# Attention scores of a hybrid block: two heads side by side on 64 rows of the array each, the causal mask added to the key terms by GpSimd

## The chip, the cores and the metric

The program runs on one core of a Trainium2 chip (8 cores, on two dies of four). The metric is the device time of one execution in microseconds (us). Lines L1, L2, ... are lines of the kernel's file, before the change unless the text says otherwise.

## The reference

Two blocks over 1024 tokens of width 1024, batch 1. All arrays are float32. The first block puts 16 learned tokens ahead of the sequence (1040 keys) and runs a state space model (SSD) and 16 heads of 64 of "forgetting" attention; the second runs 4 heads of differential attention (each with two parts of 64) and 8 heads of dilated attention of 64. What the change touches are the scores:

```python
# forgetting attention, c = cumulative sum of log f
s = jnp.einsum("bthd,bshd->bhts", qi, k).astype(jnp.float32) * scale
s = s + (cqi[..., :, None] - c_k[..., None, :])
s = jnp.where(kpos[None, :] <= qpos[:, None], s, -jnp.inf)
p = jax.nn.softmax(s, axis=-1).astype(v.dtype)
# differential attention: two parts c of each head
s = jnp.einsum('bqhce,bkhce->bchqk', qblk, k).astype(jnp.float32) * scale
s = s - slopes[:, None, None] * dist
a = jax.nn.softmax(s, axis=-1)
w = a[:, 0] - lam * a[:, 1]
# dilated attention: s + bias, masked, softmax, for three patterns that are merged
```

## The kernel before

**Numbers.** A float32 operand is kept as two halves, hi and lo, of a reduced float32 type (fp32r), and a product is the sum of hi*hi, hi*lo and lo*hi (`mm3`, L112 to L114). Projections (`project`) hold channels on the 128 partitions, so one strip of 128 weight columns gives the q, k or v of two heads: head 0 on partitions 0 to 63, head 1 on 64 to 127.

**Scores.** A head has 64 channels, half of the array's 128 rows. `stack_q` (L443, L444) splits a head's q or k into hi (ScalarE) and lo (VectorE), each head by instructions of its own on 64 partitions; `move_q` and `move_k` (L451, L457, L458) then copy halves by DMA to the other 64 partitions, so that one operand of 128 rows holds (hi, lo) of q, and two hold (hi, hi) and (lo, lo) of k. Two products of 128 rows give a head's scores: kx then ky (L566, L567; L1167; L1262 and L1264). Two heads take four products for each stretch of keys.

**Order.** `pipeline` writes the steps of eight query tiles of 128 tokens: A(i) are the scores, their maximum and the exponential, B(i) transposes the result (L620, L1289), C(i) multiplies by v (L599, L604, L1206, L1313). A runs two tiles ahead: A(i+2), C(i-1), B(i). `merge` interleaves these with the projections of the gate and of the next pair of heads by nominal costs, so the order on each engine is fixed when the program is built. Every engine takes its instructions in that order, and one that waits holds all behind it.

**Forgetting attention (`fox_attend`, eight pairs of heads).** Tile i sees W = 16 + 128(i+1) keys, 144 to 1040, in chunks of at most 512 columns. VectorE (L570) reads a chunk from PSUM, adds the key terms `cb` (the cumulative log gates, loaded by L543 as 1040 columns on all partitions for each head) and takes the running minimum of the negated scores; ScalarE (L573) takes the exponential. The causal mask of the last 128 columns is a third product: identity times a matrix of large numbers in bf16 (L569), added in PSUM. At the start of a pair, SyncE issues the store of the pair before (L611, it waits for y of L606) and then the two loads of `cb`. GpSimd clears vz and puts the v of the first 16 keys there (`v_meta`, L477, L483); TensorE transposes it (L487), then v (L468), and then comes A(0).

**The second block.** The differential attention (`scores`, L1167) writes a tile's 1024 columns of one head to a pair of PSUM banks, of which the pool has two; VectorE (L1169) reads each whole pair of banks. The dilated attention (L1262, L1264) has 688 columns for each tile in two pieces, each in a bank of its own. q and k come there from `norms` in `pair_project`: normed, split, and moved by DMA. In the narrow products L599 and L1313 two heads already share the array: each uses 64 of its columns.

Of the kernel before, what the change touches and what calls it, by code (L numbers as in the profile page):

```python
# [17 lines left out]
T = 1024  # L18
# [48 lines left out]
class Kern:  # L67
# [16 lines left out]
    def half(self, name):  # L84
        """512 columns; in the tail from a pool of their own"""
        if self.halfs is None:
            return self.slot(name, w=512)
        return self.halfs.tile([128, 512], F32, tag="half", name=name, bufs=11)

    def psum(self, one, two):  # L90
        """the banks of PSUM from here on: single ones and pairs"""
        if self.psx:
            self.psx.close()
        self.psx = self.ctx.enter_context(ExitStack())
        self.ps = self.psx.enter_context(self.tc.tile_pool(name="ps", bufs=1, space=bass.MemoryType.PSUM))
        self.one, self.two = one, two
# [35 lines left out]
    # weight strips, in the order in which they are used  # L132
# [63 lines left out]
    def consts(self):  # L196
# [6 lines left out]
        self.identb = cst.tile([128, 128], BF16, name="identb")  # L203
        self.maskb = cst.tile([128, 128], BF16, name="maskb")
        V.tensor_copy(out=self.identb, in_=self.ident)
        V.tensor_copy(out=self.maskb, in_=self.cm[:, 3, :])
# [11 lines left out]
    def rstd(self, out, ss, n):  # L218
        """1 / sqrt(ss / n + eps)"""
# [9 lines left out]
    def rsqrt(self, v, pool):  # L229
        """v [128, n] > 0 in place to 1/sqrt(v): a first guess from the exponent, three Newton steps"""  # L230
# [29 lines left out]
    def token_sums_T(self, t, n):  # L260
        """the sums by tokens: [128 tokens, block of 128, part, 32]"""
# [5 lines left out]
    def rows_out(self, v, n, dst):  # L267
        """v [128 tokens, n = (row, block of 128)]: rows of 1024 tokens in DRAM"""
# [56 lines left out]
    def softplus(self, x):  # L325
        """x [128, 9, n] in place to max(x, 0) + log(1 + exp(-|x|)), the logarithm by the series of artanh"""
# [16 lines left out]
    def dt_f(self):  # L343
# [21 lines left out]
        # cumulative log forget gates (negated: csp), as rows  # L365
# [31 lines left out]
    def dt_ssd(self):  # L397
        """SSD: within-chunk cumulative a*dt, decays"""
# [34 lines left out]
    def stack_q(self, src, stacks, c0, c1, scale, perm=False):  # L433
        """src [128 = two heads x 64, n] fp32; head 0: rows (hi, lo), head 1: rows (lo, hi); with perm, the
        tokens in the order of classes modulo 4"""
        nc = self.nc
        dst = classes if perm else lambda x: x
        if perm:
            src = by_class(src)
# [7 lines left out]
    def move_q(self, stacks, n):  # L447
        for j, st in enumerate(stacks):
            a, b = ((0, 64), (64, 128))[j]
            o, p = ((64, 128), (0, 64))[j]  # L450
            self.nc.sync.dma_start(out=st[0][o:p, :n].bitcast(F32), in_=st[1][a:b, :n].bitcast(F32))  # L451

    def move_k(self, stacks, n):
        for j, st in enumerate(stacks):
            a, b = ((0, 64), (64, 128))[j]
            o, p = ((64, 128), (0, 64))[j]
            self.nc.sync.dma_start(out=st[0][o:p, :n].bitcast(F32), in_=st[1][a:b, :n].bitcast(F32))  # L457
            self.nc.sync.dma_start(out=st[1][o:p, :n].bitcast(F32), in_=st[0][a:b, :n].bitcast(F32))  # L458
# [33 lines left out]
    def fox_project(self, p, st):  # L492
        nc = self.nc
        k = [(self.slot("kx", F32R), self.slot("ky", F32R)) for _ in range(2)]
        yield from self.project(("k", p), self.u1, PIECES_L if p else PIECES_P,
                                lambda ps, c0, c1: self.stack_q(ps, k, c0, c1, 1.0))
        self.move_k(k, L)
        st["k"] = k
        q = [(self.slot("qs", F32R), self.slot("qt", F32R)) for _ in range(2)]
        yield from self.project(("q", p), self.u1, PIECES_T,  # L500
                                lambda ps, c0, c1: self.stack_q(ps, q, c0 - 16, c1 - 16, -0.125))
        self.move_q(q, T)
        st["q"] = [s[0] for s in q]
        del q
# [11 lines left out]
    def silu2(self, ps, out):  # L516
        """2 * silu"""
# [5 lines left out]
    def pipeline(n, A, B, C, pre=lambda i: None):  # L523
        """stages of each of n query tiles, the scores two tiles ahead"""
# [13 lines left out]
    def fox_attend(self, p, st):  # L538
        nc, te = self.nc, self.nc.tensor
        cb = []  # L540
# [10 lines left out]
        def A(i):  # L551
# [5 lines left out]
            Ns[i] = []  # L557
            for j in range(2):
                N = self.slot("N")
                mn = self.sm.tile([128, 3], F32, tag="mn", name="mn", bufs=4)  # L560
                qt = st["q"][j][:, i * 128:(i + 1) * 128]
                for c in range(n):
                    s0, s1 = c * w, min(W, c * w + w)
                    S = self.bank()[:, :s1 - s0]
                    last = c == n - 1
                    te.matmul(S, qt, st["k"][j][0][:, s0:s1], start=True, stop=False)  # L566
                    te.matmul(S, qt, st["k"][j][1][:, s0:s1], start=False, stop=not last)  # L567
                    if last:
                        te.matmul(S[:, s1 - s0 - 128:], self.identb, self.maskb, start=False, stop=True)  # L569
# [1159 lines left out]
def _cols(v):  # L1729
    """[n*128] -> [128, n]"""  # L1730
    return v.reshape(-1, 128).T
# [70 lines left out]
```

## Time and profile before

| | |
|---|---|
| median of 3 runs | 2734.93 us (2732.89 to 2737.28) |
| profiled execution, its span | 2737.4 us |
| TensorE (PE) busy | 2670.8 us, 98% |
| weight loads (PEld) | 2264.5 us, 83% |
| VectorE (DVE) | 1377.0 us, 50% |
| ScalarE (ACT) | 1171.9 us, 43% |
| GpSimd (POOL) | 685.0 us, 25% |
| granted TensorE clock, mean | 0.994 |

The profile gives no time for the profiled execution beside its span, first to last instruction; it is 2.5 us above the median of the runs. A row of the timeline has the start, the duration, the engine and line, the operation, the tiles written and read, and how many instructions it merges; the duration of a matmul includes its run through the array, so the pace of a row of matmuls is read from one start to the next. In a row of groups the two numbers behind the bar are the busy time (us) and the mean duration of one (ns), then the idle time before them and what ended it.

### The profile page before, as it was taken

To read this page: it belongs to the slowest core of one execution; us is meant where nothing else is said; L and a number is where in the kernel's file an instruction comes from. 1 tells how busy PE (TensorE), PEld (TensorE's weight loads), DVE (VectorE), ACT (ScalarE), POOL (GpSimd) and SP (SyncE) were. 2 spreads that over 40 slices of the span, in tenths; PEclk is the share of its full clock that TensorE was granted. 3 is DMA by queue.
4 is the path that set the end of the run, shared out by engine and by line. 5 is a ranking of instruction groups with operands and counts; after the bars stand their busy time and mean duration, and the time that the engine had idled before them with its cause. 6 is when DMAs were issued, how large, how long until landed. Compare 5 with 4: busy or idle time off the path is not lost. (4 is left out here: it accounts for less than half of the span.)

```text
span 2737.4 us, 40266 instructions
## 1 busy us (share of the span) xinstructions
PE 2670.8 (98%) x15693; PEld 2264.5 (83%) x15693; DVE 1377.0 (50%) x2761; ACT 1171.9 (43%) x2080; POOL 685.0 (25%) x764
## 2 busy tenths in 40 slices
PE   8999999999999999999999999999999999998999
PEld 6888888889989989889887887877878877787887
DVE  5433222333474574664756777445644555446332
ACT  5444444454343443434432113445544554445331
POOL 1111111111244243342433334111111121114321
PEclk9999999999999999999999999999999999999999
DMA  3212222211123123122157654340222223324422
GB/s 124 65 57 78 71 78 78 78 47 47 70 83 118 47 85 116 49 84 108 62 186 253 215 185 161 108 130 26 85 62 78 79 79 97 98 72 138 166 67 70
DMA packets 85471, 266.98 MB, mean 98 GB/s; under 512 B 10880, under 2 KB 12032, under 8 KB 84256
## 3 DMA queue, kind: packets, MB, share of 16 engines
q1 hardware_dynamic: 85280, 264.40, 29.9%
q8 instruction: 123, 2.02, 0.3%
q14 instruction: 68, 0.56, 0.1%
HBM read 205.57 MB, written 33.49 MB: 87 GB/s over the span
## 5 line engine op out<-in xcount | busy, mean ns | idle before, releaser
L121 POOL TENSOR_TENSOR wlo<-wraw,whi 128x1024 fp32r<-128x1024 f32 (+2 forms) x168 | 374.3, 2231 | 1279.5 <-ACT whi L120 1242.6
L112 PE MATMUL bank<-uh,whi 128*128 128x512 f32 (+4 forms) x1752 | 628.4, 359 | 0.1
L114 PE MATMUL bank<-uh,wlo 128*128 128x512 f32 (+4 forms) x1752 | 619.7, 354 | 0.4 <-POOL wlo L121 0.4
L113 PE MATMUL bank<-ul,whi 128*128 128x512 f32 (+4 forms) x1752 | 619.5, 354 | 0.0
L112 PEld LDWEIGHTS bank<-uh,whi 128*128 128x128 f32 (+1 forms) x1752 | 328.9, 188 | 36.4 <-issue 3.5
L114 PEld LDWEIGHTS bank<-uh,wlo 128*128 128x128 f32 (+1 forms) x1752 | 328.6, 188 | 35.9 <-POOL wlo L121 0.9
L113 PEld LDWEIGHTS bank<-ul,whi 128*128 128x128 f32 (+1 forms) x1752 | 328.9, 188 | 32.2
L112 PE MATMUL bank<-u,whi 128*128 128x512 f32 x512 | 207.6, 405 | 0.7 <-ACT pr L931 0.7
L113 PE MATMUL bank<-u,whi 128*128 128x512 f32 x512 | 203.5, 397 | 0.0
L114 PE MATMUL bank<-u,wlo 128*128 128x512 f32 x512 | 203.2, 397 | 0.0
L120 ACT ACTIVATE whi<-wraw 128x1024 fp32r<-128x1024 f32 (+2 forms) x169 | 155.6, 927 | 24.3 <-DMA wraw<-in_w_pa_dram 15.1
L626 ACT ACTIVATE pt<-bank 128x512 f32<-128x512 f32 (+1 forms) x320 | 143.4, 507 | 37.2 <-PE bank L620 28.0
L114 PE MATMUL bank<-yh,wlo 128*128 128x512 f32 x384 | 153.0, 399 | 2.0 <-POOL wlo L121 1.9
L112 PE MATMUL bank<-yh,whi 128*128 128x512 f32 x384 | 152.8, 398 | 1.0 <-ACT whi L120 1.0
L113 PE MATMUL bank<-yl,whi 128*128 128x512 f32 x384 | 152.1, 396 | 0.0
L643 DVE SCALAR_TENSOR_TENSOR acc<-raw,cwh,acc 128x1040 f32<-128x1040 f32 x72 | 93.7, 1302 | 114.0 <-ACT acc L640 112.3
L573 ACT ACTIVATE N<-N,mn 128x272 f32<-128x272 f32 (+7 forms) x128 | 100.6, 786 | 54.3 <-DVE mn L570 51.8
L114 PEld LDWEIGHTS bank<-u,wlo 128*128 128x128 f32 x512 | 97.3, 190 | 23.0
L112 PEld LDWEIGHTS bank<-u,whi 128*128 128x128 f32 x512 | 97.6, 191 | 22.1 <-ACT pr L931 1.1
L113 PEld LDWEIGHTS bank<-u,whi 128*128 128x128 f32 x512 | 97.6, 191 | 20.6
L121 POOL TENSOR_TENSOR wo<-wl,wo 128x512 fp32r<-128x512 f32 x52 | 75.1, 1456 | 156.8 <-ACT wo L120 116.5
L620 PE MATMUL bank<-cm,N 128*128 128x128 f32 x832 | 108.2, 275 | 0.0
(326 smaller groups left out, 4997.5 us busy)
## 6 DMA issues: line engine op xcount, KB each, us to landing
wraw<-in_w_in_dram SPq DMA_DIRECT2D x120, 512.0 KB, 4.6
gt<-d_gate SPq DMA_DIRECT2D x48, 512.0 KB, 4.8
ab<-d_acs SPq DMA_DIRECT2D x32, 512.0 KB, 3.6
qs<-qt SPq DMA_DIRECT2D x48, 256.0 KB, 3.0
wl<-in_w_out_dram SPq DMA_DIRECT2D x48, 256.0 KB, 4.1
tab<-in_tab_dram SPq DMA_DIRECT2D x8, 1056.0 KB, 5.6
cb<-d_csp SPq DMA_DIRECT2D x16, 520.0 KB, 6.1
d_gate<-gt SPq DMA_DIRECT2D x16, 512.0 KB, 2.9
```

The costliest lines, as they stand in the source:

```text
L112: te.matmul(ps, lh, rh, start=start, stop=False)
L113: te.matmul(ps, lh, rl, start=False, stop=False)
L114: te.matmul(ps, ll, rh, start=False, stop=stop)
L120: self.nc.scalar.activation(out=hi, in_=src, func=AF.Copy)
L121: (self.nc.vector if vector else self.nc.gpsimd).tensor_tensor(out=lo, in0=src, in1=hi.bitcast(F32), op=ALU.subtract)
L573: nc.scalar.activation(out=N[:, :W], in_=N[:, :W], func=AF.Exp, scale=-1.0, bias=mn[:, n - 1:n], accum_out=self.lall[:, 2 * p + j, i:i + 1])
L620: nc.tensor.transpose(ps[:, b * 128:(b + 1) * 128], N[:, c:c + 128], self.ident)
L626: self.nc.scalar.activation(out=out, in_=ps, func=AF.Copy)
L643: V.scalar_tensor_tensor(out=acc[:, :L], in0=raw[:, k:k + L], scalar=w(k), in1=acc[:, :L], op0=ALU.mult, op1=ALU.add)
```

## The change

The hi and lo of q and k stay where the projection put them, head 0 on partitions 0 to 63 and head 1 on 64 to 127. `split_heads` makes hi and lo of both heads with one instruction each, and the moves by DMA are gone. `score_pair` writes three products of 64 rows for each head (hi*hi, hi*lo, lo*hi), by turns for the two heads, each to a PSUM bank of its own. The mask product L569 is gone: GpSimd makes `cmask` = `cb` plus the large numbers above the diagonal in every block of 128 keys, once for each pair of heads and ahead of `v_meta`; VectorE adds `cmask`, and after a tile GpSimd puts that tile's last 128 columns back to `cb`. The nominal costs that A returns fall from four (eight) parts to three (six). Comments and docstrings are gone as well, so line numbers shift, and a setting makes GpSimd's scratch space for DMAs smaller.

```diff
-    def stack_q(self, src, stacks, c0, c1, scale, perm=False):
...
-        for j, st in enumerate(stacks):
-            a, b = (0, 64) if j == 0 else (64, 128)
-            hi = dst(st[0][a:b, c0:c1])
-            nc.scalar.activation(out=hi, in_=src[a:b], func=AF.Copy, scale=scale)
-            nc.vector.scalar_tensor_tensor(out=dst(st[1][a:b, c0:c1]), in0=src[a:b], scalar=scale,
-                                           in1=hi.bitcast(F32), op0=ALU.mult, op1=ALU.subtract)
...
+    def split_heads(self, src, hl, c0, c1, scale, perm=False):
+        nc = self.nc
+        hi, lo = (x[:, c0:c1] for x in hl)
         if perm:
+            src, hi, lo = by_class(src), classes(hi), classes(lo)
+        nc.scalar.activation(out=hi, in_=src, func=AF.Copy, scale=scale)
+        nc.vector.scalar_tensor_tensor(out=lo, in0=src, scalar=scale, in1=hi.bitcast(F32), op0=ALU.mult,
+                                       op1=ALU.subtract)
+
+    def score_pair(self, S, q, k, start=True, stop=True):
+        for n, (a, b) in enumerate(((0, 0), (0, 1), (1, 0))):
+            for j in range(2):
+                r = slice(64 * j, 64 * j + 64)
+                self.nc.tensor.matmul(S[j], q[a][r], k[b][r], start=start and n == 0, stop=stop and n == 2)
...
     def fox_attend(self, p, st):
...
             cb.append(c)
+            m = self.ph.tile([128, L], F32, tag="cm", name="cmask", bufs=2)
+            nc.gpsimd.tensor_copy(out=m[:, 0:16], in_=c[:, 0:16])
+            r8 = lambda x: x[:, 16:].rearrange("p (b c) -> p b c", c=128)
+            nc.gpsimd.tensor_tensor(out=r8(m), in0=r8(c), in1=self.cm[:, 3].unsqueeze(1).to_broadcast([128, 8, 128]),
+                                    op=ALU.add)
+            cm.append(m)
         vT = st.pop("vT")
         st["vm"] = self.v_meta(vT)
...
+            for c in range(n):
+                s0, s1 = c * w, min(W, c * w + w)
+                S = [self.bank()[:, :s1 - s0] for _ in range(2)]
+                self.score_pair(S, [x[:, i * 128:(i + 1) * 128] for x in st["q"]], [x[:, s0:s1] for x in st["k"]])
+                for j in range(2):
+                    nc.vector.tensor_tensor_reduce(
+                        out=N[j][:, s0:s1], in0=cm[j][:, s0:s1], in1=S[j], scale=1.0,
+                        scalar=mn[j][:, c - 1:c] if c else HUGE, op0=ALU.add, op1=ALU.min, accum_out=mn[j][:, c:c + 1])
             for j in range(2):
...
+                if i < 7:
+                    nc.gpsimd.tensor_copy(out=cm[j][:, W - 128:W], in_=cb[j][:, W - 128:W])
...
     def scores(self, st, i, bias, scale, lsums):
...
+        S = [self.bank2() for _ in range(2)]
         for c in range(2):
+            self.score_pair([x[:, c, :] for x in S], [x[:, i * 128:(i + 1) * 128] for x in st["q"]],
+                            [x[:, c * 512:(c + 1) * 512] for x in st["k"]])
...
     def dil_attend(self, p, st):
...
+            S = [(self.bank(), self.bank()) for _ in range(2)]
+            q = [x[:, i * 128:(i + 1) * 128] for x in st["q"]]
+            self.score_pair([s[0][:, :n0] for s in S], q, [x[:, own] for x in k])
+            self.score_pair([s[1][:, :n1].rearrange("p (c e) -> p c e", e=144) for s in S], q,
+                            [classes(x[:, :T])[:, d["rest"], d["span"]] for x in k])
```

GpSimd between two pairs of the forgetting attention, in the program before (wlo is the lo half of a weight strip, vz the operand of L487, N a tile's exponentials, of which the first 16 columns go to pm):

```order
L121 TENSOR_TENSOR wlo_1457<-wraw_1350,whi_1456 128x1024
L477 MEMSET vz_1566 128x512
L483 COPY vz_1566<-vT_1455 64x16 x8
L576 COPY pm<-N_1598 128x16
L576 COPY pm<-N_1607 128x16
L121 TENSOR_TENSOR wlo_1618<-wraw_1460,whi_1617 128x1024
```

The same place in the changed program:

```order
L121 TENSOR_TENSOR wlo_1445<-wraw_1344,whi_1444 128x1024
L531 COPY cmask<-cb 128x16
L533 TENSOR_TENSOR cmask<-cb,cm 128x1024
L531 COPY cmask<-cb 128x16
L533 TENSOR_TENSOR cmask<-cb,cm 128x1024
L465 MEMSET vz_1560 128x512
L471 COPY vz_1560<-vT_1443 64x16 x8
L560 COPY cmask<-cb 128x128
L564 COPY pm<-N_1592 128x16
L560 COPY cmask<-cb 128x128
L564 COPY pm<-N_1593 128x16
L121 TENSOR_TENSOR wlo_1614<-wraw_1448,whi_1613 128x1024
```

Four instructions that read `cb` now stand ahead of the two that make vz, and a copy from `cb` stands ahead of each copy to pm.

TensorE at a tile of the forgetting attention with W = 656 (two chunks of 328), in the program before:

```order
L566 MATMUL bank<-kx_1205,qs_1342 128x328
L567 MATMUL bank<-ky_1206,qs_1342 128x328
L566 MATMUL bank<-kx_1205,qs_1342 128x328
L567 MATMUL bank<-ky_1206,qs_1342 128x328
L569 LDWEIGHTS identb
L569 MATMUL bank<-maskb,identb 128x128
L566 MATMUL bank<-kx_1207,qs_1344 128x328
L567 MATMUL bank<-ky_1208,qs_1344 128x328
L566 MATMUL bank<-kx_1207,qs_1344 128x328
L567 MATMUL bank<-ky_1208,qs_1344 128x328
L569 LDWEIGHTS identb
L569 MATMUL bank<-maskb,identb 128x128
```

And in the changed one (L586 is the product with v, x2 the two heads):

```order
L446 MATMUL bank<-kh_1213,qh_1338 128x328 x2
L446 MATMUL bank<-kl_1214,qh_1338 128x328 x2
L446 MATMUL bank<-kh_1213,ql_1339 128x328 x2
L446 MATMUL bank<-kh_1213,qh_1338 128x328 x2
L446 MATMUL bank<-kl_1214,qh_1338 128x328 x2
L446 MATMUL bank<-kh_1213,ql_1339 128x328 x2
L586 MATMUL bank<-pt_1742,vtok_1577 64x128
```

Eight products and two masks have become twelve products in six pairs, one of each pair for either head.

SyncE at the same place between two pairs, before and then in the changed program:

```order
L457 DMA kx_1205<-ky_1206 64x1040
L458 DMA ky_1206<-kx_1205 64x1040
L457 DMA kx_1207<-ky_1208 64x1040
L458 DMA ky_1208<-kx_1207 64x1040
L144 DMA wraw_1350<-in_w_in_dram 128x1024
L451 DMA qs_1342<-qt_1343 64x1024
L451 DMA qs_1344<-qt_1345 64x1024
L144 DMA wraw_1460<-in_w_in_dram 128x1024
L611 DMA d_yatt<-y_809 128x1024
L543 DMA cb<-d_csp 128x1040 x2
```

```order
L144 DMA wraw_1219<-in_w_in_dram 128x1024
L144 DMA wraw_1344<-in_w_in_dram 128x1024
L144 DMA wraw_1448<-in_w_in_dram 128x1024
L598 DMA d_yatt<-y_791 128x1024
L528 DMA cb<-d_csp 128x1040 x2
```

The moves are gone; the loads of `cb` still stand behind the store of y.

## Rows read from the trace of the kernel before

**Rows 1.** The page, part 1: busy time and share of each engine.
```profile
PE 2670.8 (98%) x15693; PEld 2264.5 (83%) x15693; DVE 1377.0 (50%) x2761; ACT 1171.9 (43%) x2080; POOL 685.0 (25%) x764
```

**Rows 2.** Groups by line and shape, and TensorE's waits (total, times, longest).
```profile
L1262 PE MATMUL bank<-qs,qs 128*128 128x400 f32 x48 | 19.5, 405 | 13.6 <-DMA qs<-qt 9.0 <-DVE zs L520 2.6 <-ACT vtok L469 2.0
...
PE bank L566 <- DVE mn L570: 1.3, 1, 1.3
```

**Rows 3.** Timeline of TensorE, a forgetting tile with W = 656, two chunks.
```profile
330.66 0.40 PE L566 MATMUL bank<-kx,qs 128*128 128x328 f32 x1
...
331.36 0.23 PE L569 MATMUL bank<-maskb,identb 128*128 128x128 bf16 x1
331.39 0.39 PE L566 MATMUL bank<-kx,qs 128*128 128x328 f32 x1
331.63 0.31 PE L567 MATMUL bank<-ky,qs 128*128 128x328 f32 x1
...
332.08 0.23 PE L569 MATMUL bank<-maskb,identb 128*128 128x128 bf16 x1
332.24 0.66 PE L599 MATMUL bank<-pt,vtok 128*64 128x128 f32 x8
332.83 0.87 PE L620 MATMUL bank<-cm,N 128*128 128x128 f32 x6
```

**Rows 4.** Timeline of TensorE, the product with v of a later tile.
```profile
344.56 1.31 PE L599 MATMUL bank<-pt,vtok 128*64 128x128 f32 x20
345.80 1.53 PE L620 MATMUL bank<-cm,N 128*128 128x128 f32 x12
```

**Rows 5.** Chain of waits: start, time from piece to piece, differential attention.
```profile
2143.11 1.78 PE bank L1206 x16
...
2145.77 1.86 PE bank L1167 x8
```

**Rows 6.** Timeline of POOL, SyncE and TensorE, start of a forgetting pair.
```profile
305.04 0.53 POOL L477 MEMSET vz<- 128x512 f32 x1
305.62 1.26 POOL L483 COPY vz<-vT 64x16 f32<-64x16 f32 x8
...
307.00 0.33 SPq L611 DMA_DIRECT2D d_yatt<-y  x1
307.38 1.26 SPq L543 DMA_DIRECT2D cb<-d_csp  x2
...
313.68 0.60 PE L487 MATMUL bank<-cm,vz 128*128 128x128 f32 x4
```

**Rows 7.** One line each: L543 (issues of all pairs, landing) and L487 (first, last start).
```profile
L543 SPq DMA_DIRECT2D cb<-d_csp x16: 326/444/977, 76.8 to 617.8; - x16
DMA to landing us min/median/max: 4.2/6.1/6.2
...
L487 PE MATMUL bank<-cm,vz x32: 270/272/273, 77.8 to 623.9; 128*128 128x128 f32 x32
```

**Rows 8.** Groups of GpSimd by line and shape.
```profile
L740 POOL TENSOR_TENSOR h<-h,E 128x512 f32<-128x512 f32 x28 | 29.5, 1052 | 0.0
L576 POOL COPY pm<-N 128x16 f32<-128x16 f32 x128 | 25.3, 198 | 287.1 <-ACT N L573 286.0
L782 POOL TENSOR_TENSOR zq<-zq,zq 128x1024 f32<-128x1024 f32 x6 | 14.4, 2404 | 29.3 <-ACT zq L780 29.0
```

**Rows 9.** TensorE after a wait, and windows: PE, PEld, DVE, ACT, POOL busy, PEclk, DMA.
```profile
1447.11 0.79 PE L114 MATMUL bank<-yh,wlo 128*128 128x512 f32 x1 [1.57 <-POOL wlo L121]
...
1447.20:1453.10 5.90, 5.90 (x14) 4.64 (x15) 4.64 (x5) 1.58 (x2) 1.81 (x1) 0.50 1.03 286
...
2300.40:2306.40 6.00, 6.00 (x16) 4.98 (x17) 1.10 (x4) 2.61 (x5) 4.32 (x15) 0.50 0.32 126
```

**Rows 10.** Differential attention, tiles 1 and 2 in a row, and VectorE's reads.
```profile
1943.64 0.50 PE L1167 MATMUL bank<-qs,qs 128*128 128x512 f32 x1 [0.40 <-DVE mn L1169]
...
L1169 DVE CUSTOM_DVE_ANT_0 N<-dist,bank 128x1024 f32<-128x1024 f32 x64 | 75.6, 1217 | 42.1 <-PE bank L1167 42.1
```

More of the change, by code (lines that the diff above doesn't have):

```diff
@@ L202, in consts @@
         V.memset(self.w32[:, 2:3], 1.0)
[L203 to L206, printed above, removed]
         self.ones = cst.tile([128, 128], F32, name="ones")
@@ L493, in fox_project @@
         nc = self.nc
-        k = [(self.slot("kx", F32R), self.slot("ky", F32R)) for _ in range(2)]
+        st["k"] = k = [self.slot(x, F32R) for x in ("kh", "kl")]
         yield from self.project(("k", p), self.u1, PIECES_L if p else PIECES_P,
[L496 to L499, printed above, removed]
+                                lambda ps, c0, c1: self.split_heads(ps, k, c0, c1, 1.0))
+        st["q"] = q = [self.slot(x, F32R) for x in ("qh", "ql")]
         yield from self.project(("q", p), self.u1, PIECES_T,
[L501 to L504, printed above, removed]
+                                lambda ps, c0, c1: self.split_heads(ps, q, c0 - 16, c1 - 16, -0.125))
         vT = self.slot("vT")
@@ L539, in fox_attend @@
         nc, te = self.nc, self.nc.tensor
-        cb = []
+        cb, cm = [], []
         for j in range(2):
@@ L556, in A @@
             w = -(-W // (2 * n)) * 2
-            Ns[i] = []
-            for j in range(2):
[L559 to L569, printed above, removed]
-                    nc.vector.tensor_tensor_reduce(
-                        out=N[:, s0:s1], in0=cb[j][:, s0:s1], in1=S, scale=1.0,
-                        scalar=mn[:, c - 1:c] if c else HUGE, op0=ALU.add, op1=ALU.min, accum_out=mn[:, c:c + 1])
-                nc.scalar.activation(out=N[:, :W], in_=N[:, :W], func=AF.Exp, scale=-1.0, bias=mn[:, n - 1:n],
+            N = Ns[i] = [self.slot("N") for _ in range(2)]
@@ new lines, in A @@
+            mn = [self.sm.tile([128, 3], F32, tag="mn", name="mn", bufs=4) for _ in range(2)]
+            for c in range(n):
[6 more added lines that the diff above has]
+                        scalar=mn[j][:, c - 1:c] if c else HUGE, op0=ALU.add, op1=ALU.min, accum_out=mn[j][:, c:c + 1])
@@ L578, in A @@
-            return 4 * max(W, 512) / 2.4
+                nc.gpsimd.tensor_copy(out=M[i // 4][:, 0, c:c + 16], in_=N[j][:, 0:16])
+            return 3 * max(W, 512) / 2.4
         def B(i):
@@ L1076, in norms @@
                 yield
-            for i, (x, scale, move) in enumerate(((kr, 1.0, self.move_k), (qr, sc, self.move_q))):
+            for i, (x, scale) in enumerate(((kr, 1.0), (qr, sc))):
                 next(steps)
-                o = [(self.slot("qs", F32R), self.slot("qt", F32R)) for _ in range(2)]
-                self.stack_q(x, o, 0, T, scale, dil)
-                move(o, T)
-                st["kq"[i]] = o
+                o = st["kq"[i]] = [self.slot(n, F32R, T) for n in ("qh", "ql")]
+                self.split_heads(x, o, 0, T, scale, dil)
                 yield
@@ L1109, in pair_project @@
             run(on.get(c, ()))
-        st["q"] = [s[0] for s in st["q"]]
     def v_by_tokens(self, n, st):
@@ L1156, in pair_finish, with scores @@
         yield 100
-    def scores(self, st, j, i, bias, scale, lsum):
-        nc, te = self.nc, self.nc.tensor
-        N = self.slot("N", w=T)
-        mn = self.sm.tile([128, 3], F32, tag="mn", name="mn", bufs=4)
+    def scores(self, st, i, bias, scale, lsums):
+        nc = self.nc
         o = 896 - 128 * i
-        S = self.bank2()
+        S = [self.bank2() for _ in range(2)]
         for c in range(2):
-            for v in range(2):
-                te.matmul(S[:, c, :], st["q"][j][:, i * 128:(i + 1) * 128], st["k"][j][v][:, c * 512:(c + 1) * 512],
-                          start=v == 0, stop=v == 1)
-        nc.vector.tensor_tensor_reduce(
-            out=N, in0=bias[:, o:o + 1024], in1=S.rearrange("p a b -> p (a b)"), scale=scale, scalar=HUGE,
-            op0=ALU.add, op1=ALU.min, accum_out=mn[:, 0:1])
-        nc.scalar.activation(out=N, in_=N, func=AF.Exp, scale=-1.0, bias=mn[:, 0:1], accum_out=lsum)
-        return N
+            self.score_pair([x[:, c, :] for x in S], [x[:, i * 128:(i + 1) * 128] for x in st["q"]],
+                            [x[:, c * 512:(c + 1) * 512] for x in st["k"]])
+        P = []
+        for j in range(2):
+            N = self.slot("N", w=T)
+            mn = self.sm.tile([128, 3], F32, tag="mn", name="mn", bufs=4)
+            nc.vector.tensor_tensor_reduce(
+                out=N, in0=bias[:, o:o + 1024], in1=S[j].rearrange("p a b -> p (a b)"), scale=scale, scalar=HUGE,
+                op0=ALU.add, op1=ALU.min, accum_out=mn[:, 0:1])
+            nc.scalar.activation(out=N, in_=N, func=AF.Exp, scale=-1.0, bias=mn[:, 0:1], accum_out=lsums[j])
+            P.append(N)
+        return P
     def diff_attend(self, p, st):
@@ L1182, in A @@
             l0 = self.lall[:, p, i:i + 1]
-            P = [self.scores(st, j, i, self.dist, DIFF_SLOPES[p], l[:, 1:2] if j else l0) for j in range(2)]
-            Ws[i] = (P, l, l0)
-            return 8 * 216
+            Ws[i] = (self.scores(st, i, self.dist, DIFF_SLOPES[p], (l0, l[:, 1:2])), l, l0)
+            return 6 * 216
         def pre(i):
@@ L1258, in A @@
                 mn = self.sm.tile([128, 3], F32, tag="mn", name="mn", bufs=4)
-                S = self.bank(), self.bank()
-                q = st["q"][j][:, i * 128:(i + 1) * 128]
-                for v in range(2):
-                    te.matmul(S[0][:, :n0], q, k[j][v][:, own], start=v == 0, stop=v == 1)
-                for v in range(2):
-                    te.matmul(S[1][:, :n1], q, classes(k[j][v][:, :T])[:, d["rest"], d["span"]], start=v == 0,
-                              stop=v == 1)
                 for c, (at, tab, n) in enumerate(((d["own_at"], d["tab_own"], n0), (d["rest_at"], d["tab_rest"], n1))):
                     V.tensor_tensor_reduce(
-                        out=N[:, at:at + n], in0=bias[j][:, tab:tab + n], in1=S[c][:, :n], scale=1.0,
+                        out=N[:, at:at + n], in0=bias[j][:, tab:tab + n], in1=S[j][c][:, :n], scale=1.0,
                         scalar=mn[:, 0:1] if c else HUGE, op0=ALU.add, op1=ALU.min, accum_out=mn[:, c:c + 1])
@@ L1272, in A @@
                 Ns[i].append(N)
-            return 8 * 145
+            return 6 * 145
         def B(i):
```

19 lines of the change are left out of this document (3 added, 16 removed).

## The prediction

> **What bounds the kernel now.** I read the busy times first: TensorE is busy for 98% of the span and no other engine for more than half [rows 1]. So an edit is worth what it takes from or adds to TensorE's own row of work, and a wait on that row costs its full length. Then I read TensorE's waits. They are few; the largest in a stage that the change touches is that of the first scores of the dilated pairs: 13.6 us in all, named as the moves qs<-qt (9.0) and as VectorE and ScalarE (4.6) [rows 2]. In the forgetting attention TensorE waited once, 1.3 us [rows 2].
>
> Next is the price of a column. Eight score products of 512 columns follow each other in 1.86 us, 0.2325 us each, 0.454 ns a column [rows 5]. A tile with W = 656 has eight products of 328 columns and two masks; 328 columns are 0.149 us, and the loads of their weights cost no time of their own in that pace. From the first mask to the second product behind it there are 0.27 us (331.36 to 331.63) where one product alone would take 0.15, so this mask costs 0.12; the second adds about 0.06 beside the change of mode that follows it anyway [rows 3].
>
> Two narrow products side by side can be seen in L599, 64 columns of the array for each head: 8 records take 0.59 us [rows 3] and 20 take 1.24 (344.56 to 345.80) [rows 4]. The difference is 12 records in 0.65 us, 0.054 each, while 16 full-width records of the same 128 columns take 1.78, 0.111 each [rows 5]. So two heads on two halves of the array's columns run at once, at full gain. And 8 records at 0.054 would be 0.43 us; the other 0.16 is the price of changing the way the array is divided [rows 3]. No row has two products on two halves of its rows.
>
> **The change, part by part.** All sums are against the profiled execution, 2737.4 us, which stands 2.5 us above the median of the runs.
>
> *Columns.* The score stretches are 8 x 4736 columns (forgetting), 32 x 1024 (differential) and 32 x 688 (dilated), 92,672 for each head. Four products become three pairs. A pair costs between one product (both at once) and two (one after the other). I take one, since the narrow products are the nearest row. Gain: 92,672 x 0.454 ns = **42.1 us**.
>
> *Masks.* 64 tiles x 0.18 us = **11.5 us** gained.
>
> *Changes of mode.* In the program's order the pairs stand in 112 blocks. Each is entered from full-width work, and after 55 of them full-width work follows; the other 57 are followed by narrow work, whose change is paid today too. That makes 167 new changes. Bounds: nothing, and 0.25 us (the 0.16 of the narrow products, and 0.09 for weights twice as wide). I take 0.18: **30 us** lost.
>
> *Banks in the differential attention.* Both heads of a tile now need both pairs of banks at once, and their last products end together. Where tiles 1 and 2 follow each other, tile 2 waited 0.40 us for VectorE today [rows 10]. Now both reads of 1.217 us [rows 10] begin only when tile 1 is through, and tile 2 gets its second bank pair 2.5 us later; some 0.9 of that is made up by the shorter tile. About 1.5 us at each of four places: **6 us** lost (bounds 0 and 15). Between single tiles stand 16 records and 8 transposes, about 2.7 us, which covers those reads.
>
> *Splits and moves.* Half as many instructions on ScalarE and VectorE, and 96 DMAs fewer on SyncE's queue. In the forgetting and the differential attention TensorE works on through them, so they are worth nothing there. In the dilated pairs they stand in front of the first scores: the waits of **13.6 us** go [rows 2]. Nothing is late in their place, since the chain loses more (a move's landing and half of the splits) than TensorE waited. With the second of these waits goes a stretch at half rate, the lower of TensorE's two clock levels (1.2 against 2.4 GHz): 6.0 us at 0.50 of the clock [rows 9], 3 us lost. For all four pairs I take **6 us** (bounds 3 and 10).
>
> *The mask on GpSimd.* This is the term that decides. Today GpSimd makes vz as soon as v is there, long before TensorE's L487 needs it (305.04 to 306.88, used from 313.68) [rows 6]. In the changed program four instructions that need `cb` stand ahead of vz on GpSimd's queue. The loads of `cb` are issued at 307.38, since SyncE keeps them behind the store of y, issued at 307.00 [rows 6]; that order has not changed. They land 6.1 us after issue [rows 7], at 313.5. Then GpSimd needs twice a copy of 16 columns (0.2) and an addition of 1024 columns with two operands (2.40) [rows 8], the clearing of vz (0.53) and its eight copies (1.26) [rows 6]: 7.0 us, to about 320.6. Behind L487 stand the transposes of v, the first scores and the gate's projection, all on TensorE's own queue, so nothing fills the gap: 7.0 us at each of seven pairs. At the first pair `cb` is issued at 76.8 and L487 comes at 77.8 [rows 7], so that wait is near 12 us, of which 1.3 is waited today [rows 2]: 10.5. Together **60 us**. Bounds: landing in 4.2 us [rows 7] and additions at twice the 1.05 us of 512 columns [rows 8] give 41; nothing excludes 70, if the additions meet VectorE's work.
>
> *The clock behind these waits.* After a wait of 1.57 us TensorE ran at 0.50 of the clock for 5.9 us, 14 products where full rate does 25 [rows 9]; that costs about 2.7 us. A wait of 7 us should do this too, with a part of the slow stretch inside the wait. I take 2.4 us at each of eight: **19 us** (bounds 0 and 24).
>
> *Copies back to `cb`.* 112 copies of 128 columns, between 0.2 us (16 columns) [rows 8] and 0.3 each (2.40 us for 1024 columns of an addition). VectorE's next tile waits for them, and the second head's copy stands behind ScalarE's exponential. TensorE is two tiles ahead of what VectorE makes, which covers a wait of about 1 us. I take nothing; if that cover is gone, 1 us for each pair, 8 us.
>
> *Sum.* -42.1 - 11.5 + 30 + 6 - 13.6 - 6 + 60 + 19 = +42. That is 2779 us for the profiled execution and, 2.5 lower, **2777 us** for the median. This case alone would range from 2742 to 2822.
>
> **The rivals.**
>
> *The heads don't overlap* (the change doesn't do what it says): products on two halves of the rows run one after the other. Each of the pairs then costs one product more, 3 x 92,672 x 0.454 ns = 126 us: 2903. Against it speak the narrow products, which overlap fully. For it, that no row shows halves of rows, and that both halves here write all 128 partitions of PSUM.
>
> *Weight loads stand outside.* 1440 products in 720 pairs each load weights of their own, 128 columns, at the pace of a 128-column record 0.11 us. If the two loads of a pair follow each other, a pair can't take under 0.22 us, which costs about 36 us (chunks under 490 columns): 2813. If loads for a half must wait until that half has streamed, 720 x 0.11 = 79 us: 2856. For full-width products the rows speak against it: 0.149 us for 328 columns leaves no room for a load.
> The Trainium skill (TensorE: Matmul & The Clock Gate, Part 3: Packing small matmuls) says that loads overlap matmuls in flight only where the row groups differ; two products in turn for one half have the same rows. By that rule it would be 2856, by the rows 2777. The same part gives 3.07 times for four tiles of 32 rows; spread evenly, a pair would take some 1.15 of one product (an estimate from that page), 19 us more.
>
> *The key terms are there in time* (faster): if `cb` landed 7 us before TensorE reaches L487, the wait and its slow clock would be gone and 79 us with them: 2698. The place is the issue of L543: it would have to come before about 300.4 instead of 307.38. For it: SyncE loses the moves, and `cb` has two buffers for two heads that are read for the last time a tile earlier. Against it: the store of y stands ahead and waits for a result of the last tile. It decides from a wait of under 2.7 us at each pair with its clock (37 us of gain over eight pairs, with 2 us of slow clock each); GpSimd's fixed work behind the landing is longer than that.
>
> **How the numbers follow.** The forecast has 0.74, heads without overlap 0.07, loads outside 0.13 (0.09 in turn, 0.04 beyond the streams), terms in time 0.06. The range 2738 to 2835 leaves out the no-overlap case, the terms in time, the dearer loads and 0.03 at the forecast's own ends: 0.20. A measurement tells 0.2%, 5.5 us, from no change. Slower by more than that: 0.90, from all but the last rival and the cheapest end of the forecast (0.03 within, 0.01 faster). Faster 0.07, same 0.03.
>
> **What would show it.** Right: a wait of about 7 us in front of L475's transposes in each forgetting pair, put down to GpSimd's copies to vz, with half clock behind it; two products of L446 starting together, and pairs 0.23 us apart at 512 columns; no wait at the first dilated scores; blocks of scores shorter than today but with a late first product. Wrong: L475 without a wait, or pairs at 0.3 us and more.

## The result and the profile after

The changed kernel takes 2808.02 us (median of 4 runs, 2806.88 to 2810.42) where the kernel before took 2736.11 (2732.89 to 2738.41) beside it: a ratio of 1.0263, 95% interval 1.0249 to 1.0278. It is slower, as forecast, inside the range, and 31 us above the predicted time. The profiled spans are 2805.1 and 2737.4 us, 67.7 apart. All line numbers from here on are those of the changed kernel, unless an experiment is named.

The busy times, the first view of the page (beside [rows 1]), and its row for the loads of `cb`:

```profile
PE 2679.3 (96%) x16045; PEld 2241.5 (80%) x16045; DVE 1322.8 (47%) x2703; ACT 1122.3 (40%) x2024; POOL 754.1 (27%) x908
...
cb<-d_csp SPq DMA_DIRECT2D x16, 520.0 KB, 5.9
```

TensorE is busy for 8.5 us more, in spite of fewer columns, and from its first product on its gaps sum to 115 us instead of 56. The idle time is read from TensorE's waits (line, what released it: us in all, times, longest):

```profile
PE bank L475 <- POOL vz L471: 46.3, 8, 10.4
PE bank L586 <- ACT pt L613: 21.7, 16, 1.7
...
PE bank L446 <- DVE mn L1154: 8.0, 8, 1.4
...
PE bank L446 <- ACT vtok L457: 0.8, 1, 0.8
PE bank L446 <- ACT lr L269: 0.8, 1, 0.8
```

The first row is the wait that the prediction was built on: eight times, once in each forgetting pair. The second, two waits in each pair, nobody had forecast. L446 are the new scores: 8.0 us behind VectorE's reductions are the bank waits of the differential attention; the two waits of 0.8 are all that is left of the 13.6 us in front of the dilated scores [rows 2].

The timeline of one joint between two forgetting pairs, beside [rows 6, 7, 8] (start, duration, engine and line):

```profile
335.75 0.33 SPq L598 DMA_DIRECT2D d_yatt<-y  x1
336.19 1.20 SPq L528 DMA_DIRECT2D cb<-d_csp  x2
...
341.51 0.20 POOL L531 COPY cmask<-cb 128x16 f32<-128x16 f32 x1 [9.07 <-DMA cb<-d_csp]
341.66 2.35 POOL L533 TENSOR_TENSOR cmask<-cb,cm 128x1024 f32<-128x1024 f32 x1
...
344.11 2.34 POOL L533 TENSOR_TENSOR cmask<-cb,cm 128x1024 f32<-128x1024 f32 x1
346.38 0.52 POOL L465 MEMSET vz<- 128x512 f32 x1
346.97 1.25 POOL L471 COPY vz<-vT 64x16 f32<-64x16 f32 x8
...
347.86 1.11 PE L475 MATMUL bank<-cm,vz 128*128 128x128 f32 x4 [5.29 <-POOL vz L471]
```

GpSimd can start 5.3 us after the issue, when the first of the two `cb` is there (5.9 is the median over both loads); it needs 6.35 us from there to the first finished values, and TensorE stands for 5.29 us. The stretches around it, by windows (window: length, TensorE busy with so many matmuls, granted clock, DMA share, GB/s):

```profile
336.00:342.50 6.50, 6.50 (x42) 1.00 0.86 277
346.60:353.40 6.80, 5.54 (x23) 0.50 0.00 0
353.40:357.80 4.40, 4.40 (x20) 1.00 0.02 4
```

TensorE comes out of the wait at the lower of its two levels, 1.2 instead of 2.4 GHz, and works 5.54 us so.

The wait that was not forecast, in the timeline of the same pair (W = 656, the tile shape of [rows 3]):

```profile
371.00 0.42 PE L446 MATMUL bank<-kh,qh 64*128 64x328 f32 x2
371.25 0.31 PE L446 MATMUL bank<-kl,qh 64*128 64x328 f32 x2
371.40 0.31 PE L446 MATMUL bank<-kh,ql 64*128 64x328 f32 x2
...
371.74 0.69 DVE L503 SCALAR_TENSOR_TENSOR zs<-zs,bank 128x512 f32<-128x512 f32 x1 [8.47 <-ACT zs L502]
...
372.34 0.49 DVE L555 CUSTOM_DVE_ANT_0 N<-cmask,bank 128x328 f32<-128x328 f32 x1
372.68 0.87 PE L607 MATMUL bank<-cm,N 128*128 128x128 f32 x6
...
373.65 0.55 DVE L555 CUSTOM_DVE_ANT_0 N<-cmask,bank,mn 128x328 f32<-128x328 f32 x1
373.76 0.84 ACT L561 ACTIVATE N<-N,mn 128x656 f32<-128x656 f32 x1 [2.06 <-DVE mn L555]
...
374.61 0.83 ACT L561 ACTIVATE N<-N,mn 128x656 f32<-128x656 f32 x1
...
375.43 0.85 ACT L613 ACTIVATE pt<-bank 128x384 f32<-128x384 f32 x2
...
375.95 0.32 PE L586 MATMUL bank<-pt,vtok 128*64 128x128 f32 x1 [1.14 <-ACT pt L613]
```

The transposes L607 are through by 373.6, and ScalarE is idle for 2.06 us until 373.76. But the evacuations L613 that TensorE needs next stand behind the two exponentials of a later tile on ScalarE's queue; those wait for four reductions on VectorE, and those for the gate's `zs`, which comes only when the projection is done.

Two things changed in front of this chain. The block of scores at 371.00 is over in 1.1 us, where the same tile took 1.6 before (330.66 to 332.24 [rows 3]). And the order on TensorE is another one. In the kernel before, 24 products of the gate's projection stand between the scores of W = 528 and the first product with v:

```profile
324.16 0.48 PE L112 MATMUL bank<-uh,whi 128*128 128x512 f32 x1
...
329.88 0.44 PE L599 MATMUL bank<-pt,vtok 128*64 128x128 f32 x4
```

In the changed kernel that product comes straight behind the scores, and the projection behind it:

```profile
360.63 0.40 PE L446 MATMUL bank<-kh,ql 64*128 64x264 f32 x2
362.71 0.60 PE L586 MATMUL bank<-pt,vtok 128*64 128x128 f32 x4 [1.69 <-ACT pt L613]
...
363.66 0.78 PE L112 MATMUL bank<-uh,whi 128*128 128x512 f32 x1
```

It is so in all eight pairs. The lower nominal cost that A returns moves the projection: with four parts again, the changed program has it back in its old place. No run measured that. The first of the two waits of a pair (1.4 to 1.7 us, 13.3 of the 21.7 us) stands where the projection was: scores and transposes in front of it took 3.05 us before (321.11 to 324.16) and 2.9 now (358.14 to 361.02), so the shorter blocks alone don't explain it. The second (0.6 to 1.1 us, 8.4 in all) comes one tile behind the projection. From the projection's end to that product TensorE had 5.4 us of work before and has 3.8 now; 0.8 of this are the product with v and the transposes that now stand ahead of the projection, and 1.0 the shorter blocks.

### The profile page after: what moved, and what is told of

The parts are those of the page before. It is cut to its first block, busy times and chain, and to the rows that moved or that the text cites. A ratio compares the mean times of both kernels' runs of the same rounds, so it can differ in the third digit from the quotient of the medians.

```text
span 2805.1 us, 40594 instructions
## 1 busy us (share of the span) xinstructions
PE 2679.3 (96%) x16045; PEld 2241.5 (80%) x16045; DVE 1322.8 (47%) x2703; ACT 1122.3 (40%) x2024; POOL 754.1 (27%) x908
## 3 DMA queue, kind: packets, MB, share of 16 engines
q8 instruction: 126, 2.06, 0.3%
## 4 chain that ended last, share of the span: by engine, by line
PE 87%; DVE 4%; ACT 3%; DMA 3%; POOL 2%; issue 2%; SPq 0%; DVEq 0%; POOLq 0%; ACTq 0%
PE bank L112 22%; PE bank L114 22%; PE bank L113 22%; PE bank L446 4%; PE bank L607 3%; PE bank L586 3%; PE bank L1191 2%; DMA cb<-d_csp 1%; PE bank L737 1%; PE bank L1296 1%; PE bank L734 1%; POOL cmask L533 1%; PE bank L281 1%; ACT N L561 1%; PE bank L456 1%
## 5 line engine op out<-in xcount | busy, mean ns | idle before, releaser
L613 ACT ACTIVATE pt<-bank 128x512 f32<-128x512 f32 (+1 forms) x320 | 143.7, 507 | 23.4 <-PE bank L607 15.6
L555 DVE CUSTOM_DVE_ANT_0 N<-cmask,bank 128x272 f32<-128x272 f32 (+7 forms) x128 | 58.1, 490 | 138.7 <-PE bank L446 128.9
```

The costliest lines, as they stand in the source:

```text
L555: nc.vector.tensor_tensor_reduce(out=N[j][:, s0:s1], in0=cm[j][:, s0:s1], in1=S[j], scale=1.0, scalar=mn[j][:, c - 1:c] if c else HUGE, op ...
L613: self.nc.scalar.activation(out=out, in_=ps, func=AF.Copy)
```

## The experiments

**1. The values first.** GpSimd makes `vz` and then `cmask`:

```diff
+        vT = st.pop("vT")
+        st["vm"] = self.v_meta(vT)
+        for c in cb:
             m = self.ph.tile([128, L], F32, tag="cm", name="cmask", bufs=2)
...
-        vT = st.pop("vT")
-        st["vm"] = self.v_meta(vT)
```

> The values are made ready ahead of the mask on GpSimd's queue; nothing else differs from the changed kernel. Theory (the waits in front of the value transposes L475 are GpSimd's order of work alone): those waits, 46.3 us, fall under 3 us, and the half-rate time behind them goes with them (36 us of TensorE's busy time at half rate, 18 us lost): 2808 - 46 - 18 = 2744, between 2738 and 2752; the waits L586 <- pt (21.7 us) stay. Rival (the masked key terms are needed just as soon: the first reductions on VectorE wait for them and hold the banks): the wait comes back at the first scores or at L586, and the time stays above 2775.

Measured: 2748.87 us (ratio to before 1.0038, 1.0023 to 1.0053), 59 under the changed kernel. No wait for `vz` is left. The other wait stands; the waits view of this run:

```profile
PE bank L587 <- ACT pt L614: 21.3, 16, 1.7
...
PE bank L608 <- ACT N L562: 2.5, 1, 2.5
```

The joint's wait is GpSimd's order of work. The masked terms are needed later than the values. The last row is in the first pair, and there it is not `cmask` that TensorE waits for (timeline of this run, and L334 by `--source`, here and, as L338, in the kernel before):

```profile
77.28 2.38 POOL L536 TENSOR_TENSOR cmask<-cb,cm 128x1024 f32<-128x1024 f32 x1
80.00 2.39 POOL L536 TENSOR_TENSOR cmask<-cb,cm 128x1024 f32<-128x1024 f32 x1
84.33 0.30 DVE L556 CUSTOM_DVE_ANT_0 N<-cmask,bank 128x144 f32<-128x144 f32 x1
...
L334 DVE SCALAR_TENSOR_TENSOR dt<-dt,dt x14: 307/384/2691, 56.8 to 82.7; 128x144 f32<-128x144 f32 x7, 128x288 f32<-128x288 f32 x7
...
L338 DVE SCALAR_TENSOR_TENSOR dt<-dt,dt x14: 308/384/459, 59.2 to 82.3; 128x144 f32<-128x144 f32 x7, 128x288 f32<-128x288 f32 x7
```

`cmask` is ready at 82.39, and VectorE comes to its first reduction only at 84.33, without an idle moment before it. Two of its instructions for the SSD (L334) began 13 and 21 ns behind GpSimd's two additions and lasted 2.69 us, to 0.3 us past the end of these, instead of 0.46. So GpSimd's additions held VectorE for 4.5 us, and all behind it.

**2. The exponentials behind the evacuations.** `exps(i + 2)` holds the copies back, the exponentials and the copies to `pm`, and is called at the end of B(i):

```diff
             del Ns[i]
+            if i + 2 in E:
+                exps(i + 2)
             return 2 * (i + 1) * 109
```

> In the forgetting attention the exponentials of tile i+2 (with the copies back and the copies to pm) are issued behind the evacuations of tile i's transposes, no longer in front of them. Theory (the waits L586 <- pt, 21.7 us, are ScalarE's order of work: an evacuation that is ready stands behind exponentials that wait for VectorE's reductions): the waits at L586 fall under 4 us, the half-rate stretches behind them (23 us busy at half rate, 11 us lost) go too: 2808 - 20 - 11 = 2777, between 2770 and 2785. Rival (VectorE's reductions are late whatever the order, so that the exponentials and then the transposes L607 wait instead): L607 <- N takes over most of the 21.7, and the time stays above 2795.

Measured: 2781.52 us, 26.5 under the changed kernel (1.0159, 1.0144 to 1.0174). Of the waits for `pt` in the forgetting attention 2.3 us are left, no transpose waits in their place, and the joint is as it was:

```profile
PE bank L475 <- POOL vz L471: 47.7, 8, 10.5
...
PE bank L596 <- ACT pt L623: 2.3, 7, 0.3
```

**3. No copies back.**

```diff
-                if i < 7:
-                    nc.gpsimd.tensor_copy(out=cm[j][:, W - 128:W], in_=cb[j][:, W - 128:W])
```

> The copies that take the mask off again (cmask<-cb, 128 columns, 112 of them) are left out, so that later tiles see the mask on older diagonal blocks and their weights are not those of the reference. Theory (ScalarE's order and a shorter score block make the L586 waits; the copies hold a reduction by 0.2 us now and then): the waits at L586 shrink from 21.7 to between 15 and 20, time 2798 to 2808. Rival (the copies back make the waits): L586 falls under 6 us and the time to 2775 to 2785.

Measured: 2812.89 us (1.0273, 1.0256 to 1.029). The wait hardly moves:

```profile
PE bank L584 <- ACT pt L611: 21.3, 16, 1.6
```

The copies, which the prediction had named as the thing that might lose its cover, cost TensorE next to nothing; the expected 15 to 20 us of waits and 2798 to 2808 us of time were both missed, on the side of no effect. The time is even 5 us higher; the profile of this run has more of TensorE's busy time at half rate (92 us against 76).

**4. The pairs alone, with the mask on TensorE.** In `fox_attend` no `cmask`, and behind each tile's last chunk

```diff
+                    for j in range(2):
+                        te.matmul(S[j][:, s1 - s0 - 128:], self.identb, self.maskb, start=False, stop=True)
```

> The three pairs of products stay, but the mask is added by TensorE as in the kernel before and GpSimd makes no cmask: the pairs alone. Theory: the waits at L475 go with their half rate (-46 - 18), the 128 masks come back (+11.5 and up to 3 for changes of mode), the L586 waits shrink a little since a block is 0.3 us longer (15 to 20 left): 2808 - 64 + 13 - 4 = 2753, between 2744 and 2762: still slower than before by the L586 waits, which eat what the pairs gain. Rival (the mask on GpSimd is all that is wrong; pairs alone gain 42 - 30 + 13.6 + 6 = 31): about 2705.

Measured: 2742.98 us, 1.0020 (1.0010 to 1.0029) of before, 1 us under the expected range. The waits for `pt`, at 15.0 us, belong to the pairs and their nominal costs, which this kernel keeps, and not to the mask on GpSimd.

**5. The mask alone**, in the kernel before:

```diff
-                    if last:
-                        te.matmul(S[:, s1 - s0 - 128:], self.identb, self.maskb, start=False, stop=True)
...
-                        out=N[:, s0:s1], in0=cb[j][:, s0:s1], in1=S, scale=1.0,
+                        out=N[:, s0:s1], in0=cm[j][:, s0:s1], in1=S, scale=1.0,
```

> The kernel before, stacked scores and moves and all, with only its masks moved: GpSimd makes cmask as in the changed kernel, in front of the values. Theory (the two halves of the change are separate): the waits before the value transposes come here too, 45 us and 18 of half rate, the masks' 11.5 go, and the waits of the first products with the weights pt do not come, since a stacked block is long enough: 2737 + 45 + 18 - 11.5 = 2788, between 2778 and 2800. Rival (the copies back hold VectorE here as well, or the waits need the shorter blocks of the pairs): above 2805 or below 2765.

Measured: 2796.77 us, 1.0220 (1.0203 to 1.0237), 61 us over before, inside the expected range. Waits view, by lines of this kernel:

```profile
PE bank L487 <- POOL vz L483: 47.4, 8, 10.5
...
PE bank L1267 <- DMA qs<-qt: 9.2, 6, 2.8
```

No wait for `pt` in the forgetting attention; this kernel has the blocks, the nominal costs and the place of the projection of the kernel before. So the mask costs 61 us and the pairs 6 (experiment 4), together 67, and the whole change 72: the halves nearly add.

**6. Experiments 1 and 2 together.**

> The values first on GpSimd's queue (v_first) and the exponentials behind the evacuations (exps_late) together. Theory (two separate waits, each with its own half rate): the gains add, 2808 - 59 (measured with the first) - 26 (with the second) = 2723, between 2714 and 2730, which is under the kernel before. Rival (the two waits cover for one another, so that one grows when the other goes): 2735 or more.

Measured: 2719.93 us, 0.9935 (0.9921 to 0.9948): the gains add, and the kernel is faster than before.

**7. The pairs without their wait**: experiment 4 with the exponentials behind the evacuations.

> Pairs with the mask on TensorE (2743.0 measured) and the exponentials behind the evacuations. Theory: the 15.0 us of waits for pt that are left there go, with 2 of half rate: 2726, between 2720 and 2732; the pairs alone are then worth some 11 us against the kernel before, about what the dilated waits give (13.6 + 3), since their columns (42) are used up by changes of mode (33 to 41) and bank waits (8). Rival (the pairs themselves gain, and other waits hide it): below 2715.

Measured: 2721.49 us, 0.9943 (0.9928 to 0.9958), 21 under experiment 4. Here the mask is still TensorE's, and the time is that of experiment 6. The mask products do cost some 10 us in the forgetting score blocks (96.1 against 86.0 in experiment 6, from the record ahead of each block to the second one behind, waits and half rate taken out), but experiment 6 has 5.0 us more idle time and loses 5.6 more to half rate. Of the idle time 3.8 lie in the first pair (4.9 against 1.1), where GpSimd's additions hold VectorE (experiment 1).

**8. More changes of mode**, on the kernel of experiment 6 (the same in `scores`):

```diff
+                if c:
+                    te.matmul(S[0][:, :128], st["q"][0][:, i * 128:(i + 1) * 128], st["k"][0][:, s0:s0 + 128],
+                              start=True, stop=True)
                 self.score_pair(S, [x[:, i * 128:(i + 1) * 128] for x in st["q"]], [x[:, s0:s1] for x in st["k"]])
```

> As the combined kernel, with one product over all 128 rows (128 columns, its result overwritten) put in front of each later chunk of the forgetting and the differential scores, 80 of them: each adds a change out of the pairs' mode and one into it. Theory (a change costs 0.20 us, as entries and exits read in the trace): 80 x (0.40 + 0.06 to 0.11 for the product) = 37 to 41 us more than the combined kernel, less some 5 where TensorE waits for VectorE anyway. Rival (what is paid at a block's edge is the wait for something else, a bank or the read of the result before, and not the change): 5 to 10 us more, the products alone.

Measured: 2752.08 us, 32.2 over experiment 6: 0.40 us for each of the 80 places, product included. The change itself is what costs. It can be seen in one differential block of the changed kernel (timeline of TensorE; each row merges the products of two heads, which start 2 to 9 ns apart):

```profile
1926.74 0.60 PE L456 MATMUL bank<-cm,vT 128*128 128x128 f32 x4
1927.27 0.50 PE L446 MATMUL bank<-qh,qh 64*128 64x512 f32 x2
1927.61 0.40 PE L446 MATMUL bank<-ql,qh 64*128 64x512 f32 x2
1927.84 0.39 PE L446 MATMUL bank<-qh,ql 64*128 64x512 f32 x2
1928.07 0.39 PE L446 MATMUL bank<-qh,qh 64*128 64x512 f32 x2
1928.30 0.40 PE L446 MATMUL bank<-ql,qh 64*128 64x512 f32 x2
1928.53 0.39 PE L446 MATMUL bank<-qh,ql 64*128 64x512 f32 x2
1928.85 0.50 PE L112 MATMUL bank<-u,whi 128*128 128x512 f32 x1
```

In the block a pair follows a pair after 0.23 us, the time of one full-width product [rows 5]: full overlap. The first step takes 0.34 and the step out 0.32: about 0.1 too much each. As much again lies in front of the first pair and behind the first full-width product; over all blocks the medians are 0.094 and 0.106 on the way in, 0.095 and 0.106 on the way out to full width.

**9. Head by head.** As experiment 6, with the two loops of `score_pair` exchanged:

```diff
-        for n, (a, b) in enumerate(((0, 0), (0, 1), (1, 0))):
-            for j in range(2):
+        for j in range(2):
+            for n, (a, b) in enumerate(((0, 0), (0, 1), (1, 0))):
```

> As the combined kernel, but in every chunk the three products of one head stand before the three of the other, so that only the products at a change of head can run together. Theory (two halves of the rows run at once; loads of weights for the half that streams are hidden as for full-width products): a block of n chunks takes 4n + 1 products' time instead of 3n, 92,672 + 46,400 columns at 0.454 ns = 63 us more than the combined kernel, 2775 to 2795. Rival 1 (halves never overlap and the records 3 ns apart are an artefact): no difference, since the same six products run one after the other. Rival 2 (the skill's rule, TensorE: Matmul & The Clock Gate, Part 3: Packing small matmuls: a load waits while its own row group streams): four loads of each chunk stand open, 960 loads at 0.06 to 0.11 us, another 58 to 106 us on top, 2840 to 2890.

Measured: 2722.1 us, 0.9940 (0.9926 to 0.9953), the same as experiment 6. Theory and second rival both fail; the first rival gives the right time for a wrong reason. The same block in this kernel, where the program has head 0's three products ahead of head 1's:

```profile
1832.46 0.51 PE L446 MATMUL bank<-qh,qh 64*128 64x512 f32 x2
1832.80 0.41 PE L446 MATMUL bank<-ql,qh 64*128 64x512 f32 x2
1833.03 0.40 PE L446 MATMUL bank<-qh,ql 64*128 64x512 f32 x2
...
1834.05 0.50 PE L112 MATMUL bank<-u,whi 128*128 128x512 f32 x1
```

The pairs are there again, at the same pace, the second record 7 to 19 ns behind the first. Twelve products of 512 columns one after the other would take 2.8 us and took 1.6; and if a product on 64 rows just took half the time, starts would lie 0.12 us apart and in the program's order. So head 1's first product ran beside head 0's first, past two that the program has in front of it, as compiled too. That every engine takes its instructions in the program's order, as said ahead of the prediction, does not hold here.

**10. Differential scores stacked again**, on experiment 6: `stack_q`, the moves and the old `scores` for n < 4.

> As the combined kernel, but the differential attention has its stacked scores back, with the splits and moves of the kernel before. Theory (there the pairs gain nothing: 32 x 1024 columns at 0.454 ns are 14.9 us, 64 changes of mode at 0.2 us take 12.8 back, and the waits of 8.0 us for VectorE with the half rate behind them are a loss): about 10 us under the combined kernel, 6 to 16. Rival (the pairs gain there too, the splits and moves weighing on the joints): slower than the combined kernel by 3 us or more.

Measured: 2712.7 us, 0.9910 (0.9896 to 0.9924), 7 under experiment 6. This is the fastest version. The bank waits of 8.0 us are 1.6 there.

**11. Pairs in the dilated attention alone**, masks on GpSimd behind the values.

> Pairs only in the dilated attention, stacked scores in the other two, masks on GpSimd behind the values and the exponentials where they were. Theory (pairs gain next to nothing by themselves; what gains are the masks, 11.5, and the dilated waits with their half rate, 16.6): 2737 - 28 = 2709, between 2702 and 2717, the same as or under the version that keeps pairs in the forgetting attention too (2712.7). Rival (the forgetting pairs are worth their columns, 17 us): 2720 or more.

Measured: 2724.19 us, 0.9956 (0.9941 to 0.9971): a miss, 15 us too slow, and the rival's case. Against experiment 10 the profile has 5.2 us more in the forgetting score blocks (91.1 against 85.9, measured as in experiment 7), 4.0 more idle time and 3.7 of half rate. So the forgetting pairs are worth some 5 us of blocks, not their 17 of columns and not nothing. And of the 12 us of idle time that went from the dilated scores, three waits of the first forgetting pair gave 5.5 back (the kernel before has 1.3 there).

## Why the prediction was right, and where it was 31 us short

The sum, step by step, against the profiles. The first row is measured over the 112 score blocks, from the start of the record ahead to that of the second one behind, without idle time and without what half rate costs: 221.8 us before, 202.1 after. Half rate is the busy time at 0.50 of the clock, halved.

| step | forecast, us | measured, us |
|---|---|---|
| columns, masks, changes of mode | -23.6 | -19.7 |
| bank waits, differential | +6 | +6.4 (8.0 less 1.6) |
| dilated waits | -13.6 | -12.0 |
| half rate there and elsewhere | -6 | -5.8 |
| GpSimd in front of L475 | +60 | +45.0 (46.3 less 1.3) |
| half rate behind these waits | +19 | +18.1 |
| waits for `pt` at L586 | 0 | +21.7 |
| half rate behind those | 0 | +11.5 |
| sum | +42 | +65.2 of 67.7 |

- **Columns and modes: right.** Pairs run at one product's time, the change costs 0.20 where 0.18 was taken. 167 changes at 0.20 take 33 of the 42 us of columns. The pairs alone lose 0.2% with the waits for `pt` (experiment 4) and gain 0.6% without them (experiment 7).
- **The rivals.** No overlap, loads outside and key terms in time did not come. The rule of the Trainium skill (TensorE: Matmul & The Clock Gate, Part 3: Packing small matmuls), that a load runs beside matmuls in flight only where the row groups differ, would have made 2856 us; the trace disagrees. In a differential block of experiment 9 the loads for the next pair begin 2 and 3 ns behind the starts of the two products in flight, one on each half, and last 0.18 us, inside these products' 0.39; pairs stay 0.23 apart.
- **The mask on GpSimd: right mechanism, size 15 too high.** Experiments 1 and 5 show it from both sides. GpSimd started 5.3 us after the issue, not 6.1, since it needs only the first of the two loads to start and 6.1 was the median of both; the chain behind took 6.35, not 7.0. The wait was 4.7 to 5.9 in seven pairs, and 10.4 in the first, forecast as 7.0 (6.8 by the forecast's own rows) and near 12.
- **The step that failed** is "TensorE is two tiles ahead of what VectorE makes, which covers a wait of about 1 us. I take nothing; if that cover is gone, 1 us for each pair". The cover was looked for behind the copies, which cost nothing (experiment 3). What had lost its cover was the chain of `zs`, reductions, exponentials and evacuations: 33 us with half rate. The forecast took the place of every other piece of TensorE's work as given, though the nominal costs that set it had changed, and booked every microsecond taken out of a score block as gain, without asking which other engine's work it had been hiding. Experiments 2, 4, 5 and 7 place it: it comes with the pairs' half of the change, and goes when the evacuations are issued first. How much of it is the projection's new place and how much the shorter blocks is not shown by a run: every kernel with pairs in the forgetting attention also has the new order. By the traces the first wait of each pair, with all the half rate behind it, some 25 of the 33 us, goes with the projection's place, and the second with both.

About 2.5 us of the difference are not assigned.

## What to carry to other kernels

Before an engine's stage is made shorter, or a cost that orders the program is changed, list what other engines do during that stage, what moves in the order, and who waits next; on queues that work in order, an evacuation that TensorE needs soon belongs ahead of an exponential that is needed two tiles later. Work that waits for a late load goes behind work on the same queue that does not. Two heads on two halves of the rows give full overlap, but 0.2 us at each change of mode eats most of that in blocks of three to nine short pairs: here they lost 7 us in the differential attention (experiment 10), left some 5 in the forgetting attention, and paid best where they also saved something else, the moves in front of the dilated scores.

## What the runs showed of the hardware

Products on the two halves of the rows do not keep the program's order with each other: with three products of head 0 in front of three of head 1, the first two started 10 ns apart and the block took the same time (experiment 9). Waits of 4.7 to 5.9 us were followed by 2.8 to 5.6 us of busy time at 0.50 of the clock. In six of eight pairs the first of the two waits for `pt`, 1.7 us, was followed by 3.1 to 6.3 us of it too; the second, 0.6 to 1.1 us, never was. Of the 96 us that the two kinds of wait cost, 30 were lost to the lower clock and not to the waits themselves. Two VectorE instructions of 0.46 us that began just behind additions of GpSimd lasted 2.69 us, to the end of these (experiment 1).
